# Fixed order of the last value projections: weights two units ahead, four decay buffers, output-weight halves in the gate stage, key norms one unit on

## The chip, the cores and the metric

The kernel runs on one core of one Trainium2 chip. The metric is the device time of one execution in microseconds (us). Before the change the median of three executions is 2239.89 us (2238.68 to 2241.77).

## The reference

One inference step of a two-layer streaming encoder, over 2048 prompt tokens and 32 sample tokens (2080 in all), width 1024: a gated delta layer, then a layer of sliding-window attention. Only the first layer's input side matters here:

```python
A_HEADS = 8; A_DK = A_DV = 128; CONV_W = 4
proj = x @ w_in                       # q, k, v: 24 rows of 128 features; gate z: 8 rows; decay and beta: 16 columns
qkv, conv_state = causal_conv(proj[..., :3072], buf, w)   # 4 taps per feature, then SiLU
q, k = l2norm(q), l2norm(k)
gcum = jnp.cumsum(g, axis=-1)
decay = jnp.exp(jnp.where(incl, gcum[..., :, None] - gcum[..., None, :], -jnp.inf))
# ... chunks of tokens: (I + lower)^-1, recurrence over chunks, o
out = (rms_norm(o) * silu(z)) @ w_out
```

## The kernel before

All large matrix products are made in three passes: each operand is split into a high part (a rounded copy, made on ACT) and a low part (the difference, made on POOL or DVE), and `project` multiplies hi by hi, hi by lo and lo by hi over eight slices of 128 (lines 74 to 82).

**Units.** A unit is one of the 24 rows of 128 features of q (0 to 7), k (8 to 15) and v (16 to 23), over all 2080 tokens in five blocks of 416. A block is 24 matmuls into one PSUM buffer, which ACT copies into the row R (`block`, line 294); a unit is 120 matmuls. There are six such PSUM buffers. `conv` (line 196) is a generator that turns the finished row of the unit before into its convolved, activated form on ACT and DVE: a scaled copy on ACT (L204), three multiply-adds on DVE (L207), a tanh on ACT (L211), a last DVE pass (L213), then the stores to scratch on SP's queue (L216, L218); for q and k also squares, a transpose and a sum (L221 to L224), and behind the last key unit the norms of all keys (`norms`, with its table of logarithms, some 40 small DVE instructions and eight matmuls at L456).

**Weights.** `fetch_weights` (L47) loads a unit's 512 KB into the one buffer `w_raw`; `split_fetched` makes `w_hi` on ACT (L54) and `w_lo` on POOL (L55), two buffers each.

**Orders.** The rest of the program around this is put in order by a list scheduler. Units 0 to 15 are free (FREE = 15). From unit 16 on, `ordered` (L230) fixes the order of TensorE, DVE, ACT and SP to that in which the code issues: per unit the fetch of the next unit's weights, then per block one step of the decay table, some steps of `conv`, and the block; the next weights are split behind block 0, and behind block 2 comes one output-weight half.

**Decays.** `decays` (L260) makes the exponentials of the differences of cumulative gates, 17 token tiles of two head groups, so 34 steps: a broadcast load into E (L271), a mask added on DVE (L280), four exponentials on ACT (L284), a store (L285). Three places serve as E in turn, and a step's load goes out one step ahead.

**Output weights.** `split_out_weights` (L1074) splits a_w_out once into hi and lo halves kept in scratch, 16 steps of a load (256 KB, L1080), a cast on ACT (L1081), a subtraction on POOL (L1082) and a store (512 KB, L1083), through the buffer `th`, which `conv` uses too. Eight steps stand in units 7 to 14, eight in units 16 to 23.

**Gate stage.** `z` (L301) makes the eight rows of the gate for blocks 0 to 2; it yields after every six matmuls, four times a block, 96 steps in all. Thirteen steps are interleaved with the convolution of unit 23, then 15 follow, then `Ahead.inverses` begins, which needs k, E and other tables from scratch and makes the inverses of the first two chunks: key products on TensorE (L669), then a chain of small DVE instructions (L703, L705), interleaved with gate steps. TensorE and DVE have a fixed order there; ACT, POOL and SP are scheduled. Gate rows leave through `keep_gate` on SP (L328, L333).

Of the kernel before, what the change touches and what calls it, by code (L numbers as in the profile page):

```python
# [10 lines left out]
F32 = mybir.dt.float32  # L11
# [8 lines left out]
ET = mybir.EngineType  # L20
# [71 lines left out]
def drain(gen):  # L92
    for _ in gen:
        pass


class P1:
# [50 lines left out]
    def qkv(self):  # L148
        nc, I, T, G, big, one = self.nc, self.I, self.T, self.G, self.big, self.one
        G["triu"] = one.tile([128, 128], F32, tag="triu", name="triu")  # L150
        nc.sync.dma_start(G["triu"][:], I["triu"])
        G["ones"] = one.tile([128, 128], F32, tag="ones", name="ones")
        nc.gpsimd.memset(G["ones"][:], 1.0)
        gtmp = one.tile([128, 8, NTT, H], F32, tag="gtmp", name="gtmp")
        G["cc"] = gtmp[:, 3]
        abT = gtmp[:, 0:2].rearrange("p a t h -> p (a t h)").rearrange("p (t c) -> p t c", c=16)
        abr = one.tile([48, NT], F32, tag="th", name="abr")
        nc.gpsimd.memset(abT[:, NTT - 1, :], 0.0)
        wab = self.wab
        Rs = [self.row(0), self.row(1)]  # L160
        for b in range(NB):
            ps = self.ps()
            xh, xl = self.x[b]
            for k in range(KC):
                nc.tensor.matmul(ps[:48, :TB], wab[:, k, :48], xh[:, k, :], start=(k == 0), stop=False,
                                 skip_group_check=True)
                nc.tensor.matmul(ps[:16, :TB], wab[:, k, :16], xl[:, k, :], start=False, stop=(k == KC - 1),
                                 skip_group_check=True)
            nc.scalar.copy(abr[:, b * TB:(b + 1) * TB], ps[:48, :TB])
            for t in range(b * TB // 128, NTT if b == NB - 1 else (b + 1) * TB // 128):  # L170
                n = min(128, NT - t * 128)
                tp = self.pt.tile([128, 512], F32, tag="tp", name="tp")
                nc.tensor.transpose(tp[:n, :48], abr[:, t * 128:t * 128 + n], G["ident"][:48, :48])
                nc.vector.tensor_copy(abT[:n, t, :], tp[:n, 32:48])
                nc.vector.tensor_tensor(out=abT[:n, t, :], in0=abT[:n, t, :], in1=tp[:n, :16], op=ALU.add)
            for i in range(2):
                self.block(Rs[i], self.w0[i], b)
        gates(nc, I, T, G, abT, gtmp, one, self.pt)
        parts = one.tile([128, 8, NT // 32], F32, tag="parts", name="parts")
        wo = split_out_weights(nc, one, "th", I["a_w_out"], T["wo"])  # L180
        for i in range(self.FREE + 1):
            if i < 2:
                R = Rs[i]
            else:
                w = split_weights(nc, self.wp, I["w_in"][i], nc.gpsimd)
                R = self.row(i)
                for b in range(NB):
                    self.block(R, w, b)
            if 7 <= i < self.FREE:
                next(wo)  # L190
            if i < self.FREE:
                drain(self.conv(i, R, parts))
        with self.tc.manual_schedule(engines={ET.PE, ET.DVE, ET.Activation, ET.SP}):
            self.ordered(R, parts, wo)

    def conv(self, i, R, parts):

# [29 lines left out]
        if h == 7:  # L227
            norms(nc, self.G, parts, self.sel, kind, one, self.pt)

    def ordered(self, R, parts, wo):  # L230

        nc, I = self.nc, self.I
        w = split_weights(nc, self.wp, I["w_in"][self.FREE + 1], nc.gpsimd)
        matrices = None
        for i in range(self.FREE + 1, 24):
            c = self.conv(i - 1, R, parts)
            nxt = self.row(i)
            raw = fetch_weights(nc, self.wp, I["w_in"][i + 1])
            next(c)
            for b in range(NB):  # L240
                if matrices:
                    next(matrices, None)
                for _ in range((2, 2, 1, 1, 0)[b]):
                    next(c, None)
                if b == 3:
                    next(wo)
                self.block(nxt, w, b)
                if b == 0:
                    following = split_fetched(nc, self.wp, raw, nc.gpsimd)
            drain(c)  # L250
            R, w = nxt, following
            if i == self.FREE + 1:
                matrices = self.decays()
                next(matrices)
        self.room = self.one, ("parts", "gtmp")
        self.tail = self.conv(23, R, parts)
        next(self.tail)
        self.w24 = w

    def decays(self):  # L260

        nc, G, T = self.nc, self.G, self.T
        nm = self.one.tile([128, 128], F32, tag="triu", name="nm")
        nc.sync.dma_start(nm[:], self.I["nm"])
        todo = [(t, q) for t in (NTT - 1, *range(NTT - 1)) for q in range(2)]

        def load(m):
            t, q = todo[m]
            n, hs = min(128, NT - t * 128), slice(q * 4, q * 4 + 4)
            E = self.one.tile([128, 4, 128], F32, tag=("parts", "sel", "gtmp")[m % 3], name="E")  # L270
            nc.sync.dma_start(E[:, :, :n], T["gcum"][t, hs, :n].partition_broadcast(128))  # L271
            return E, t, n, hs

        ahead = load(0)
        yield
        for m in range(len(todo)):
            E, t, n, hs = ahead
            if m + 1 < len(todo):
                ahead = load(m + 1)
            nc.vector.tensor_tensor(out=E[:n, :, :n], in0=E[:n, :, :n],  # L280
                                    in1=nm[:n, :n].unsqueeze(1).to_broadcast([n, 4, n]), op=ALU.add)
            for j in range(4):
                h = hs.start + j
                nc.scalar.activation(E[:n, j, :n], E[:n, j, :n], AF.Exp, bias=G["ngc"][:n, t, h:h + 1])  # L284
            nc.sync.dma_start(T["E"][t, :n, hs, :n], E[:n, :, :n])  # L285
            yield

    def row(self, i):
# [782 lines left out]
        yield  # L1071


def split_out_weights(nc, pool, tag, src, kept):  # L1074

    for k in range(kept.shape[1]):
        for c in (slice(0, D // 2), slice(D // 2, D)):
            t = pool.tile([128, 3, D // 2], F32R, tag=tag, name="wo_parts")
            raw = t[:, 0].bitcast(F32)
            nc.sync.dma_start(raw, src[k][:, c])  # L1080
# [560 lines left out]
def program(tc, I, O, T, G):  # L1641
    nc = tc.nc
# [16 lines left out]
    chunks[0].pool = zp  # L1659
    ahead = Ahead(tc, mid, left, I, O, T, G).inverses(chunks[:2])  # L1660
    next(ahead)
    with tc.manual_schedule(engines={ET.PE, ET.DVE}):
        for _ in range(15):
            next(z)
        for i, _ in enumerate(ahead):
            if i < 8 or i % 2:
                next(z, None)
        drain(z)
    w = p1.first_gate(nc.gpsimd)
    raw = p1.late_raw(zp, 1)  # L1670
    mid.close()
# [225 lines left out]
```

## Time and profile before

| | |
|---|---|
| median of three executions | 2239.89 us |
| the profiled execution | 2244.03 us, span 2242.2 us |
| TensorE matmul busy | 2158.0 us, 96% of the span |
| VectorE (DVE), ScalarE (ACT), GpSimd (POOL) busy | 62%, 40%, 37% |
| mean granted TensorE clock | 0.985 |
| DMA, mean over the span | 137 GB/s |
| units 16 to 23 and the first gate steps | about 399 to 681 us of the span |

How to read the rows: times are us from the start of the span; "L54" is a line of the kernel; `out<-in` names tiles; a bracket at the end of a row gives how long the engine sat idle before it and which instruction, on which engine, ended the wait. SPq rows are DMA issues in the order of SP's queue. In rows of stretches, the count in parentheses is of instructions; a few matmul records can be missing. PEld is the load of a stationary operand, which overlaps the matmuls.

### The profile page before, as it was taken

Reading aid. Unit: us, or ns where it says so; the run is one execution under the profiler, and the core shown is the slowest. Engines: PE = TensorE matmul, PEld = TensorE weight load, DVE = VectorE, ACT = ScalarE, POOL = GpSimd, SP = SyncE. Lnnn points to the kernel's source line nnn. Section 1 sums busy time; section 2 is a strip of 40 time slices with the busy share of each in tenths; the row PEclk is TensorE's granted clock in tenths of the full one; section 3 lists DMA queues with packets and bytes.
Section 4 is the critical chain, followed back from the end, with each engine's and each line's share of the span. In section 5 each row is a group of like instructions: output and inputs, shape, how many; then the busy total and the mean of one; then the engine's idle time right before and its main releaser. Section 6 shows DMA issues by size and latency. Waiting matters only on the chain.

```text
span 2242.2 us, 36907 instructions
## 1 busy us (share of the span) xinstructions
PE 2158.0 (96%) x13690; PEld 1988.5 (89%) x13690; DVE 1387.3 (62%) x2718; ACT 899.4 (40%) x2273; POOL 833.9 (37%) x1185
## 2 busy tenths in 40 slices
PE   8999999988788999999999999999999999999998
PEld 6999999988788999999988888999999987787885
DVE  3666666744556668888887886224543225768775
ACT  4344444344441266666762212312112235544442
POOL 1422132111121157777750111236432124555654
PEclk9999999998899999999999999999999999999999
DMA  5222233254546535445765664455212277333321
GB/s 194 67 70 83 93 115 99 75 170 152 159 145 164 160 127 165 152 164 163 261 223 178 215 210 129 147 182 198 82 65 78 74 190 257 85 85 104 95 71 52
DMA packets 268116, 308.29 MB, mean 137 GB/s; under 512 B 79728, under 2 KB 198832, under 8 KB 267664
## 3 DMA queue, kind: packets, MB, share of 16 engines
q1 hardware_dynamic: 256688, 282.45, 40.6%
q10 hardware_dynamic: 11248, 23.48, 3.2%
q8 instruction: 108, 1.77, 0.3%
q14 instruction: 72, 0.59, 0.1%
HBM read 189.63 MB, written 116.60 MB: 137 GB/s over the span
## 4 chain that ended last, share of the span: by engine, by line
PE 63%; DVE 3%; DMA 2%; ACT 1%; issue 1%; SPq 0%; POOL 0%; DVEq 0%; ACTq 0%; POOLq 0%
PE ps L78 8%; PE ps L80 8%; PE ps L79 8%; PE po L1118 5%; PE po L1120 5%; PE po L1119 5%; PE ot L1611 4%; PE S L1590 2%; PE tr L1605 2%; PE g L669 1%; PE ks L811 1%; PE gq L796 1%; PE sp L811 1%; PE vp L811 1%; PE op L841 1%; PE op L835 1%
## 5 line engine op out<-in xcount | busy, mean ns | idle before, releaser
L78 PE MATMUL ps<-act_hi,w_hi 128*128 128x416 f32 x2000 | 715.4, 358 | 21.9 <-ACT w_hi L54 19.4
L80 PE MATMUL ps<-act_hi,w_lo 128*128 128x416 f32 x2000 | 713.3, 357 | 21.8 <-POOL w_lo L55 21.8
L79 PE MATMUL ps<-act_lo,w_hi 128*128 128x416 f32 x2000 | 708.7, 354 | 0.4 <-DVE act_lo L70 0.4
L78 PEld LDWEIGHTS ps<-act_hi,w_hi 128*128 128x128 f32 x2000 | 381.8, 191 | 30.7 <-ACT w_hi L54 22.3
L80 PEld LDWEIGHTS ps<-act_hi,w_lo 128*128 128x128 f32 x2000 | 381.2, 191 | 29.1 <-POOL w_lo L55 24.6
L79 PEld LDWEIGHTS ps<-act_lo,w_hi 128*128 128x128 f32 x2000 | 381.7, 191 | 5.6 <-DVE act_lo L70 0.9
L55 POOL TENSOR_TENSOR w_lo<-w_raw,w_hi 128x1024 fp32r<-128x1024 f32 x44 | 130.4, 2964 | 471.0 <-ACT w_hi L54 435.2
L207 DVE SCALAR_TENSOR_TENSOR y<-R,convw,y 128x2083 f32<-128x2083 f32 x72 | 181.7, 2524 | 43.2 <-ACT y L204 29.5
L1598 POOL TENSOR_TENSOR P<-P,sm 128x384 f32<-128x384 f32 (+2 forms) x128 | 100.5, 807 | 174.2 <-DVE sm L1476 105.5
L703 POOL TENSOR_TENSOR tm<-L,Tt 128x60 f32<-128x60 f32 (+19 forms) x365 | 124.5, 341 | 99.3 <-issue 40.2
L705 POOL TENSOR_TENSOR Tt<-Tt,tm 128x60 f32<-128x60 f32 (+19 forms) x365 | 143.7, 394 | 28.6
L1472 ACT ACTIVATE P<-S,nm 128x192 f32<-128x192 f32 (+3 forms) x260 | 104.6, 418 | 90.6 <-DVE nm L1465 43.9
L1118 PE MATMUL po<-wo_hi,g_hi 128*128 128x512 f32 x256 | 103.5, 404 | 0.0
L299 ACT COPY R<-ps 128x416 f32<-128x416 f32 (+1 forms) x144 | 60.1, 443 | 105.0 <-PE ps L80 94.0
L1120 PE MATMUL po<-wo_hi,g_lo 128*128 128x512 f32 x256 | 100.3, 392 | 0.6 <-DVE g_lo L1161 0.6
L1119 PE MATMUL po<-wo_lo,g_hi 128*128 128x512 f32 x256 | 100.0, 391 | 0.0
L1316 POOL TENSOR_TENSOR rs<-rs,sin 128x416 f32<-128x416 f32 x50 | 70.7, 1415 | 78.5 <-DVE rs L1315 72.2
L1611 PE MATMUL ot<-pt,vd 128*128 128x256 f32 x372 | 97.2, 388 | 1.6 <-ACT pt L1607 1.1
L280 DVE TENSOR_TENSOR E<-E,nm 128x512 f32<-128x512 f32 (+1 forms) x34 | 37.6, 1105 | 95.2 <-DMA s_E<-E 66.3
L1118 PE MATMUL po<-wo,g_hi 128*128 128x512 f32 x224 | 93.0, 415 | 0.0
L1401 DVE SCALAR_TENSOR_TENSOR za<-zs,za 128x416 f32<-128x416 f32 x40 | 32.2, 808 | 94.9 <-ACT za L1400 94.8
L1120 PE MATMUL po<-wo,g_lo 128*128 128x512 f32 x224 | 90.1, 402 | 0.0
(304 smaller groups left out, 4089.7 us busy)
## 6 DMA issues: line engine op xcount, KB each, us to landing
w_raw<-in_w_in SPq DMA_DIRECT2D x40, 512.0 KB
w_raw<-in_b_w_in SPq DMA_DIRECT2D x20, 512.0 KB
k<-s_k SPq DMA_DIRECT2D x17, 512.0 KB
E<-s_E SPq DMA_DIRECT2D x17, 512.0 KB
s_bz<-za SPq DMA_DIRECT2D x40, 208.0 KB
s_bq<-ra SPq DMA_DIRECT2D x40, 208.0 KB
s_q<-y SPq DMA_DIRECT2D x8, 1024.0 KB
s_wo<-wo_parts SPq DMA_DIRECT2D x16, 512.0 KB
```

What stands on the lines that cost most here:

```text
L55: sub.tensor_tensor(out=lo[:], in0=raw[:], in1=hi[:], op=ALU.subtract)
L78: nc.tensor.matmul(ps, hi[:, k, :], xh[:, k, :], start=(k == 0), stop=False)
L79: nc.tensor.matmul(ps, hi[:, k, :], xl[:, k, :], start=False, stop=False)
L80: nc.tensor.matmul(ps, lo[:, k, :], xh[:, k, :], start=False, stop=(k == KC - 1))
L207: nc.vector.scalar_tensor_tensor(out=y[:], in0=R[:, j:j + W], scalar=self.convw[:, i, j:j + 1], in1=y[:], op0=ALU.mult, op1=ALU.add)
L703: P.tensor_tensor(out=tm[:n, i0 - k:, :w], in0=L[:n, i0:, j:j + 1].to_broadcast(sh), in1=Tt[:n, j:j + 1, :w].to_broadcast(sh), op=ALU.mult)
L705: P.tensor_tensor(out=Tt[:n, i0:, :w], in0=Tt[:n, i0:, :w], in1=tm[:n, i0 - k:, :w], op=ALU.subtract)
L1118: nc.tensor.matmul(ps[:n], ghi[:, k, :n], w[0][:, k, cs], start=a, stop=False)
L1119: nc.tensor.matmul(ps[:n], ghi[:, k, :n], w[1][:, k, cs], start=False, stop=False)
L1120: nc.tensor.matmul(ps[:n], glo[:, k, :n], w[0][:, k, cs], start=False, stop=z)
L1472: nc.scalar.activation(P[u], src, AF.Exp, bias=nm[:, u:u + 1], scale=1.0, accum_out=sm[:, u:u + 1])
L1611: nc.tensor.matmul(ot[:, p], self.vd[:, kc0 + j, p, :], pt[:, 2 * j:2 * j + 2, :], start=(j == 0), stop=(j == nj - 1))
```

## The change

Weights: the fetch for unit i + 2 is issued before block 2 of unit i, and the split of unit i + 1's weights stands at the start of unit i. Decays: a fourth place for E (`gtmp` is made into two), loads three steps ahead, issued behind the step's store; the steps start in unit 17 at block 1, and two units take a second step at block 3. The norms of the keys, which were drained at the end of unit 16, are drained in unit 17 before block 1. Output-weight halves leave the fixed order: nine now stand in units 6 to 14, and seven in the gate stage with two buffers of their own. POOL's order is fixed as well in `ordered`, and 18 instead of 15 gate steps stand ahead of the inverses.

```diff
         parts = one.tile([128, 8, NT // 32], F32, tag="parts", name="parts")
-        wo = split_out_weights(nc, one, "th", I["a_w_out"], T["wo"])
+        self.parts = one, "th"
+        self.wo = split_out_weights(nc, self, I["a_w_out"], T["wo"])
...
-            if 7 <= i < self.FREE:
-                next(wo)
+            if 6 <= i < self.FREE:
+                next(self.wo)
...
-        with self.tc.manual_schedule(engines={ET.PE, ET.DVE, ET.Activation, ET.SP}):
-            self.ordered(R, parts, wo)
+        with self.tc.manual_schedule(engines={ET.PE, ET.DVE, ET.Activation, ET.SP, ET.Pool}):
+            self.ordered(R, parts)
...
         w = split_weights(nc, self.wp, I["w_in"][self.FREE + 1], nc.gpsimd)
+        raw = fetch_weights(nc, self.wp, I["w_in"][self.FREE + 2])
         matrices = None
         for i in range(self.FREE + 1, 24):
             c = self.conv(i - 1, R, parts)
             nxt = self.row(i)
-            raw = fetch_weights(nc, self.wp, I["w_in"][i + 1])
+            following = split_fetched(nc, self.wp, raw, nc.gpsimd)
             next(c)
             for b in range(NB):
-                if matrices:
+                for _ in range(2 if i in (self.FREE + 3, self.FREE + 4) and b == 3 else 1 if matrices else 0):
                     next(matrices, None)
                 for _ in range((2, 2, 1, 1, 0)[b]):
                     next(c, None)
-                if b == 3:
-                    next(wo)
+                if b == 2 and i < 23:
+                    raw = fetch_weights(nc, self.wp, I["w_in"][i + 2])
+                if i == self.FREE + 2 and b == 1:
+                    drain(last)
+                    matrices = self.decays()
+                    next(matrices)
                 self.block(nxt, w, b)
-                if b == 0:
-                    following = split_fetched(nc, self.wp, raw, nc.gpsimd)
-            drain(c)
+            last = c
             R, w = nxt, following
-            if i == self.FREE + 1:
-                matrices = self.decays()
-                next(matrices)
...
         nm = self.one.tile([128, 128], F32, tag="triu", name="nm")
+        both = self.one.tile([128, 2, 4, 128], F32, tag="gtmp", name="E")
...
-            E = self.one.tile([128, 4, 128], F32, tag=("parts", "sel", "gtmp")[m % 3], name="E")
+            if m % 2:
+                E = both[:, m // 2 % 2]
+            else:
+                E = self.one.tile([128, 4, 128], F32, tag=("parts", "sel")[m // 2 % 2], name="E")
...
-        ahead = load(0)
+        ahead = [load(0), load(1), load(2)]
         yield
         for m in range(len(todo)):
-            E, t, n, hs = ahead
-            if m + 1 < len(todo):
-                ahead = load(m + 1)
+            E, t, n, hs = ahead.pop(0)
...
             nc.sync.dma_start(T["E"][t, :n, hs, :n], E[:n, :, :n])
+            if m + 3 < len(todo):
+                ahead.append(load(m + 3))
             yield
...
-def split_out_weights(nc, pool, tag, src, kept):
+def split_out_weights(nc, room, src, kept):
...
+            pool, tag = room.parts
...
+    p1.parts = new_pool(tc, mid, "p1_wo", 2, side="right"), "wo_parts"
     with tc.manual_schedule(engines={ET.PE, ET.DVE}):
-        for _ in range(15):
+        for _ in range(18):
             next(z)
         for i, _ in enumerate(ahead):
             if i < 8 or i % 2:
                 next(z, None)
+            if i % 16 == 8:
+                next(p1.wo, None)
         drain(z)
+        drain(p1.wo)
```

In the orders below the lines of the changed kernel are a few higher (E's load is L276, its store L288, the value row's stores L217 and L219, the exponentials L287, the output-weight load and store L1086 and L1089). SP's queue in a unit of the fixed order, before, from one fetch of weights to the next:

```order
L47 DMA w_raw<-in_w_in 128x1024
...
L285 DMA s_E<-E 128x512
L216 DMA s_v<-y 128x16x128
L218 DMA s_v<-y 128x32
L1080 DMA wo_parts<-in_a_w_out 128x512
L1083 DMA s_wo<-wo_parts 128x2x512
L271 DMA E<-s_gcum 128x512
L285 DMA s_E<-E 128x512
L47 DMA w_raw<-in_w_in 128x1024
```

and with the change:

```order
L47 DMA w_raw<-in_w_in 128x1024
L288 DMA s_E<-E 128x512
L276 DMA E<-s_gcum 128x512
L288 DMA s_E<-E 128x512
L276 DMA E<-s_gcum 128x512
L217 DMA s_v<-y 128x16x128
L219 DMA s_v<-y 128x32
L288 DMA s_E<-E 128x512
L276 DMA E<-s_gcum 128x512
```

The output-weight load and store are gone from between the value row's stores and the decay loads, and a block's load of E now follows its store.

ACT's order around the cast of a unit's weights in the same part, before:

```order
L284 ACTIVATE E<-E,t_ngc 128x128 x4
L1081 CAST wo_parts<-wo_parts 128x512
L299 COPY R<-ps 128x416
L284 ACTIVATE E<-E,t_ngc 128x128 x4
L299 COPY R<-ps 128x384
L299 COPY R<-ps 128x32
L204 ACTIVATE y<-R,convw 128x2083
L284 ACTIVATE E<-E,t_ngc 128x128 x4
L299 COPY R<-ps 128x416
L54 CAST w_hi<-w_raw 128x1024
```

and with the change:

```order
L287 ACTIVATE E<-E,t_ngc 128x128 x4
L304 COPY R<-ps 128x384
L304 COPY R<-ps 128x32
L54 CAST w_hi<-w_raw 128x1024
L205 ACTIVATE y<-R,convw 128x2083
L287 ACTIVATE E<-E,t_ngc 128x128 x4
L304 COPY R<-ps 128x416
```

The cast has moved ahead of the convolution's first step and of the unit's first exponentials, right behind the copies of the row before (384 and 32 are the two pieces of its last block).

SP's queue from the last value row's store to the loads of the inverses, before:

```order
L216 DMA s_v<-y 128x16x128
L218 DMA s_v<-y 128x32
L333 DMA s_z<-z 128x64
L328 DMA s_z<-z 128x2x128
L333 DMA s_z<-z 128x96
L627 DMA tinit<-in_tinit 128x256
L640 DMA k<-s_k 128x1024
L640 DMA k<-s_k 128x8x32
```

and with the change:

```order
L217 DMA s_v<-y 128x16x128
L219 DMA s_v<-y 128x32
L47 DMA w_raw<-in_w_in 128x1024
L338 DMA s_z<-z 128x64
L333 DMA s_z<-z 128x2x128
L338 DMA s_z<-z 128x96
L632 DMA tinit<-in_tinit 128x256
L645 DMA k<-s_k 128x1024
L648 DMA E<-s_E 32x8x32
L1086 DMA wo_parts<-in_a_w_out 128x512 x2
L645 DMA k<-s_k 128x8x32
```

A fetch of gate weights, an E and two output-weight halves now stand ahead of the small load of k, which the first key product needs.

More of the change, by code (lines that the diff above doesn't have):

```diff
@@ L228, in conv, with ordered @@
             norms(nc, self.G, parts, self.sel, kind, one, self.pt)
-    def ordered(self, R, parts, wo):
+    def ordered(self, R, parts):
         nc, I = self.nc, self.I
         w = split_weights(nc, self.wp, I["w_in"][self.FREE + 1], nc.gpsimd)
+        raw = fetch_weights(nc, self.wp, I["w_in"][self.FREE + 2])
         matrices = None
```

## The prediction

> **What bounds the kernel now.** I first read who waited for whom on TensorE (waited for: us in total, times, longest), since it is busy 96% of the span.
>
> ```profile
> PE ps L80 <- POOL w_lo L55: 21.8, 7, 3.6
> PE ps L78 <- ACT w_hi L54: 19.4, 7, 3.7
> PE g L669 <- DMA k<-s_k: 11.1, 3, 9.5
> ```
>
> TensorE waits some 41 us for split weights and 11 us for one load of keys; what else it waits for is small. Next the busy times by stretch, cut where units begin (columns: PE, PEld, DVE, ACT, POOL busy with counts, granted clock, DMA share, GB/s).
>
> ```profile
> 60.00:420.00 360.00, 360.00 (x1917) 353.14 (x1916) 246.49 (x151) 156.42 (x203) 97.85 (x86) 1.00 0.29 88
> ...
> 474.00:480.00 6.00, 5.39 (x16) 5.21 (x17) 4.55 (x4) 3.79 (x7) 1.09 (x3) 0.50 0.31 77
> ```
>
> ```profile
> 446.40:470.30 23.90, 22.62 (x121) 22.14 (x119) 6.94 (x6) 11.62 (x26) 1.60 (x3) 1.00 0.61 179
> 470.30:502.00 31.70, 25.84 (x120) 24.85 (x120) 14.68 (x10) 13.77 (x30) 6.33 (x6) 0.89 0.53 159
> ...
> 598.30:630.40 32.10, 25.46 (x121) 24.47 (x121) 13.90 (x10) 13.77 (x30) 5.58 (x7) 0.89 0.49 153
> 630.40:654.30 23.90, 19.96 (x96) 18.97 (x96) 11.02 (x6) 10.02 (x21) 9.33 (x4) 0.86 0.57 159
> 654.30:681.00 26.70, 17.20 (x90) 16.76 (x90) 16.58 (x14) 8.98 (x13) 4.00 (x4) 0.89 0.55 159
> 681.00:700.00 19.00, 18.97 (x102) 18.21 (x103) 12.17 (x24) 3.42 (x6) 2.40 (x1) 0.88 0.72 193
> 700.00:785.00 85.00, 85.00 (x480) 84.14 (x479) 60.84 (x162) 18.14 (x32) 14.10 (x18) 1.00 0.48 145
> ```
>
> From 60 to 420 us TensorE runs gapless at clock 1.00. From 470 us each unit of the same 120 matmuls takes some 32 us. After 700 us it is gapless again. So all that this change can win lies between 470 and 700 us. The loss in a unit has two halves: idle time, and the clock, which is 0.50 for some 7 us behind the idle time (0.11 of 32 us is 3.5 us). Then the order of time, TensorE first (last bracket: idle before, and what ended it), and the casts that mark an undisturbed unit.
>
> ```profile
> 421.74 2.09 PE L456 MATMUL n_ps<-parts,sel 128*128 128x136 f32 x8 [0.70 <-DVE parts L224]
> ...
> 470.34 0.46 PE L78 MATMUL ps<-act_hi,w_hi 128*128 128x416 f32 x1 [1.33 <-ACT w_hi L54]
> 474.61 0.72 PE L80 MATMUL ps<-act_hi,w_lo 128*128 128x416 f32 x1 [3.63 <-POOL w_lo L55]
> ...
> 630.35 0.45 PE L78 MATMUL ps<-act_hi,w_hi 128*128 128x416 f32 x1 [3.75 <-ACT w_hi L54]
> ...
> 681.03 0.64 PE L669 MATMUL g<-k 128*32 128x32 f32 x8 [9.50 <-DMA k<-s_k]
> ```
>
> ```profile
> 353.09 1.06 ACT L54 CAST w_hi<-w_raw 128x1024 fp32r<-128x1024 f32 x1 [3.34 <-PE ps L79]
> ...
> 375.69 1.05 ACT L54 CAST w_hi<-w_raw 128x1024 fp32r<-128x1024 f32 x1 [3.34 <-PE ps L79]
> ```
>
> The two casts are one unit apart: 22.60 us. Unit 16 ends at 421.74 - 0.70 = 421.04; 470.34 is the start of unit 19 and 630.35 that of the first gate head. Why w_hi and w_lo come late is told by SP's queue, then ACT, POOL and DVE, around 455 to 475 us.
>
> ```profile
> 454.86 1.23 SPq L1080 DMA_DIRECT2D wo_parts<-in_a_w_out  x1
> 460.99 0.37 SPq L1083 DMA_DIRECT2D s_wo<-wo_parts  x1
> 461.46 0.41 SPq L271 DMA_DIRECT2D E<-s_gcum  x1
> ...
> 462.66 0.44 SPq L47 DMA_DIRECT2D w_raw<-in_w_in  x1
> ```
>
> ```profile
> 458.97 0.62 ACT L1081 CAST wo_parts<-wo_parts 128x512 fp32r<-128x512 f32 x1 [7.18 <-DMA wo_parts<-in_a_w_out]
> ...
> 461.65 2.05 ACT L204 ACTIVATE y<-R,convw 128x2083 f32<-128x2083 f32 x1
> 467.68 1.28 ACT L284 ACTIVATE E<-E,t_ngc 128x128 f32<-128x128 f32 x4 [3.98 <-DVE E L280]
> ...
> 469.25 1.04 ACT L54 CAST w_hi<-w_raw 128x1024 fp32r<-128x1024 f32 x1
> ```
>
> ```profile
> 459.67 1.29 POOL L1082 TENSOR_TENSOR wo_parts<-wo_parts 128x512 fp32r<-128x512 f32 x1 [13.58 <-ACT wo_parts L1081]
> ...
> 470.37 4.19 POOL L55 TENSOR_TENSOR w_lo<-w_raw,w_hi 128x1024 fp32r<-128x1024 f32 x1 [8.46 <-ACT w_hi L54]
> ```
>
> ```profile
> 466.95 0.69 DVE L280 TENSOR_TENSOR E<-E,nm 128x512 f32<-128x512 f32 x1 [13.36 <-DMA s_E<-E]
> ```
>
> It is one loop through four in-order engines. SP issues the output-weight half's load at 454.86; its store can go only at 460.99, after ACT's cast and POOL's subtraction. Only then come the next decay block's load and the weights' fetch (462.66). DVE gets that decay block at 466.95, ACT its exponentials at 467.68, and the weights' cast stands behind them in ACT's order: 469.25. TensorE needed it at 469.0. The loop takes 502.00 - 470.30 = 31.7 us, a unit needs 22.6: TensorE is paced by it, 9 us lost per unit.
>
> **The change part by part.**
>
> Output-weight halves leave the fixed order: eight go (one into the free part, seven into the gate stage). That takes 461.46 - 454.86 = 6.6 us of SP's standstill out of each loop. The one in the free part costs ACT 0.62 and POOL 1.29 us, where they are busy 156 and 98 of 360 us under a gapless TensorE: nothing.
>
> Weights two units ahead: the fetch goes out in the middle of a unit for the unit after next, and the cast leads each unit's ACT work instead of following an exponential. It needs a whole unit's lead to fail before TensorE waits: from fetch to cast at most 6.6 us (462.66 to 469.25, an upper bound, as ACT was busy elsewhere), cast 1.04, subtraction 4.19.
>
> Four decay buffers: a load is issued three blocks ahead (three blocks of 4.5 us) and needs the store of one block ago to have landed, so DVE's waits for E should go.
>
> Key norms one unit on: they sit on DVE behind three convolution passes of unit 17.
>
> ```profile
> 423.87 0.30 DVE L459 TENSOR_SCALAR n_x<-n_ps 128x136 f32<-128x136 f32 x1 [2.18 <-PE n_ps L456]
> ...
> 435.51 0.30 DVE L447 TENSOR_TENSOR t_ngc<-t_ngc,n_lx 128x136 f32<-128x136 f32 x1
> ...
> 467.56 4.81 DVE L207 SCALAR_TENSOR_TENSOR y<-R,convw,y 128x2083 f32<-128x2083 f32 x2
> ```
>
> They are the tightest spot, so I follow it by hand. Unit 16 ends at 421.04; copies, cast and convolution start (0.5, 1.0, 2.05) end at 424.6, three passes of 2.4 at 431.8, norms (11.9) at 443.7, the first E and its exponentials (2) at 445.7. SP puts that E's store ahead of the fetch for unit 19: fetch 446.6, raw there by 453.2, cast 454.2, subtraction 458.4. Unit 19 begins at 421.04 + 2.09 + 2 x 22.60 = 468.3: 9.9 us to spare. Norms cost TensorE their 2.09 us as before; were that cover gone, the excess would be paid once.
>
> Can the other engines keep 22.6 us? The rows of a unit give DVE 14.7, ACT 13.8 - 0.6 = 13.2, POOL 6.3 - 1.3 = 5.0 us. DMA: 0.51 of 32 us is 16.3; a half's 0.75 MB at 159/0.53 = 300 GB/s is 2.5; the 13.8 left is a share of 0.61, which unit 18 (446.4 to 470.3) had without starving TensorE until its end. So units 17 to 23 should run gapless. **The first gate head starts at 421.04 + 2.09 + 7 x 22.60 = 581.3 instead of 630.35: 49.0 us.**
>
> Gate stage up to the first keys: before, 13 + 15 = 28 gate steps (six matmuls, a twentieth of a unit, 1.13 us: 31.6 us) took 681.03 - 630.35 = 50.7 us. That is 19.0 lost to late weights, half clock and the 9.5 us for k. Now 31 steps stand there, 35.0 us. Is k in time?
>
> ```profile
> 670.21 0.37 SPq L216 DMA_DIRECT2D s_v<-y  x1
> ...
> 676.23 1.10 SPq L640 DMA_DIRECT2D k<-s_k  x2
> ```
>
> From the last value row's store to k's arrival it took 681.03 - 670.21 = 10.8 us; the new SP order puts four more issues between them (a weight fetch, E, two output-weight loads: 2.0 us at 0.5). That store is ready some 16.6 us after the stage begins: 3.6 to the convolution's first step, 4.8 for two passes, 1.3 for a gate block, 2.4, then 2.2 and 2.3 for another block and the last pass. So k lands at 29.4, 5.6 us before it is needed. If the cover goes: between nothing and the old 9.5 + 3.5 us. I take nothing. **The 19.0 us are won.** The three steps moved forward are missing later, so they cancel.
>
> The half clock behind the k wait (681 to 700 us, 0.12 x 19) is worth 0 to 2.3 more; I leave it against small waits that I cannot price.
>
> Seven halves in the gate stage: ACT 7 x 0.62 = 4.3, POOL 7 x 1.29 = 9.0, DMA 5.3 MB = 18 us at 300 GB/s, beside 85 us in which ACT is busy 18, POOL 14, and DMA 0.48: hidden as long as SP does not hold up gate stores. DVE is the close one, 60.84 of 85 us. Beside POOL's subtraction an E add took 2.83 us, not 0.68, and the subtraction 4.19, not 2.41:
>
> ```profile
> 472.28 2.83 DVE L280 TENSOR_TENSOR E<-E,nm 128x512 f32<-128x512 f32 x1
> ...
> 477.33 0.68 DVE L280 TENSOR_TENSOR E<-E,nm 128x512 f32<-128x512 f32 x1
> ```
>
> ```profile
> 639.31 2.41 POOL L343 TENSOR_TENSOR w_lo<-w_raw,w_hi 128x1024 fp32r<-128x1024 f32 x1 [4.73 <-ACT w_hi L351]
> ```
>
> So a subtraction may hold DVE for its length: bounds 0 and 9.0 us, 69.8 of 85 us at most, still under TensorE: nothing. The Trainium skill, "SBUF — State Buffer", section "Who interferes with whom", says that a VectorE instruction with two SBUF inputs and a GpSimd one that reads SBUF exclude each other for the whole instruction, whoever comes first. By that rule the full 9.0 us fall on DVE, and a stage that DVE paced would end 9.0 us later; the rows above agree with it in kind.
>
> Sum: 49.0 + 19.0 = **68.0 us**. The profiled execution took 2244.03 us for its span of 2242.2, so it would take 2176.0; it lies 4.1 over the median, 2239.89, which becomes **2171.9, say 2172**. Behind 785 us the engines' orders are unchanged.
>
> **The rivals.**
>
> A: the decay chain still paces. Without the halves the loop is 31.7 - 6.6 = 25.1 us, if the four buffers win nothing. For it: convolution, exponentials and casts are one serial chain on ACT and DVE (the row x2 of 4.81 us, 2.83 for an E add beside POOL). Against: the cast no longer stands behind an exponential of its own unit. Five units times 2.5 us is 12.5 lost: 2184.
>
> B: the gate stage gives back. The halves' loads stand in SP's queue before the small k, and a store waiting for POOL holds back gate stores and weight fetches. Against: six PSUM buffers (27 us of blocks) stand between TensorE and the stores. Price: the old k wait and its half clock, 9.5 + 3.5 = 13 us, or DVE's 9.0: 2181 to 2185.
>
> C, slower: each of the seven halves stops the gate stage as it stopped the units, 31.7 - 22.6 = 9.1 us, since the same load, cast, subtraction, store sequence stands in SP's queue, and the k wait stays: 63.7 + 9.5 = 73.2 against 68.0, 2245. It decides from 9.7 us per half. Against: no exponential waits behind it there.
>
> D: the lead is in name only. One raw buffer remains, so a fetch waits for POOL's subtraction of the previous weights; if those slipped a whole unit, the loop would stay: 2240.
>
> **How the numbers follow.** Forecast 0.68 (own range 2166 to 2178: the 2.3 us of clock and 2 us of spread above, 6 us of small waits), A 0.13, B 0.12, C 0.05, D 0.02. The range 2166 to 2190 takes in A and B. Over 0.2% (4.5 us, about what a measurement can tell from no change) faster: forecast, A and B, 0.93; within: D, 0.02; slower: C, 0.05.
>
> **What would show it.** Windows of 22.6 us with 120 matmuls at clock 1.00 from 424 to 581 us; w_hi and w_lo gone from TensorE's waits; the E waits gone from DVE's; the first key product near 616 us without a wait; about 85 us of gapless TensorE behind it. Units of 25 us mean A, a wait on k or a clock of 0.5 in the gate stage means B, gaps between gate heads C. I would be wrong altogether if the gapless stretch brought a lower clock by itself, which 360 us at 1.00 speak against.

## The result, and the profile after

| | before | after |
|---|---|---|
| median (lowest to highest), 4 executions each | 2240.83 us (2238.68 to 2242.36) | 2173.12 us (2169.78 to 2174.22) |
| the profiled execution, its span | 2244.03 us, 2242.2 us | 2172.59 us, 2170.7 us |
| start of the gate stage | 630.35 us | 580.8 us |
| first key product of the inverses | 681.03 us | 619.23 us |

The ratio is 0.9696, with a 95% interval of 0.9679 to 0.9713: 67.7 us faster, where 67.9 (2239.89 to 2172) were predicted. The page of the changed kernel, busy times:

```profile
PE 2136.9 (98%) x13690; PEld 1973.4 (91%) x13690; DVE 1369.1 (63%) x2718; ACT 898.9 (41%) x2273; POOL 837.7 (39%) x1185
```

Who waited for whom on TensorE (waited for: us in total, times, longest):

```profile
PE ps L78 <- ACT w_hi L54: 2.3, 1, 2.3
...
PE ps L80 <- POOL w_lo L55: 1.1, 1, 1.1
...
PE g L674 <- DMA k<-s_k: 0.8, 1, 0.8
```

Before, w_lo, w_hi and k headed this list with 21.8, 19.4 and 11.1 us (20.7, 16.2 and 9.5 of them between 421 and 720 us). What is left of them lies elsewhere in the program: restricted to the time from 60 to 720 us, this view is empty. The busy times by stretch (PE, PEld, DVE, ACT, POOL with counts, granted clock, DMA share, GB/s), first before, cut at the start of the gate stage and at the first key product, then after, cut at the same events, with a stretch of about one unit in between:

```profile
421.00:630.30 209.30, 175.29 (x849) 169.21 (x848) 101.96 (x93) 88.22 (x191) 39.34 (x41) 0.91 0.49 149
630.30:681.00 50.70, 37.20 (x186) 35.78 (x186) 27.69 (x20) 19.00 (x34) 13.34 (x7) 0.87 0.56 160
681.00:785.00 104.00, 103.97 (x580) 102.35 (x581) 73.02 (x185) 21.56 (x38) 16.50 (x19) 0.98 0.53 154
```

```profile
421.00:580.80 159.80, 159.80 (x848) 158.57 (x847) 99.21 (x97) 89.63 (x199) 36.11 (x33) 1.00 0.58 173
580.80:619.20 38.40, 38.40 (x205) 37.97 (x204) 19.61 (x18) 13.28 (x19) 11.18 (x7) 1.00 0.62 169
619.20:720.00 100.80, 100.80 (x577) 99.29 (x577) 68.86 (x182) 24.09 (x45) 23.70 (x24) 1.00 0.64 200
...
470.00:492.00 22.00, 22.00 (x119) 21.85 (x118) 13.51 (x10) 14.22 (x33) 5.27 (x5) 1.00 0.71 207
```

The same 848 matmuls took 209.3 us and now 159.8, without a gap and at clock 1.00. The middle row needs care: 186 matmuls stood between the start of the gate stage and the first key product before, 205 now (a matmul or two can be missing from either).

The order of time in the changed kernel, at the spot that the prediction followed by hand and then in the gate stage:

```profile
443.77 0.28 DVE L283 TENSOR_TENSOR E<-E,nm 32x128 f32<-32x128 f32 x1
...
445.97 0.38 SPq L47 DMA_DIRECT2D w_raw<-in_w_in  x1
...
450.65 1.05 ACT L54 CAST w_hi<-w_raw 128x1024 fp32r<-128x1024 f32 x1 [1.16 <-DMA w_raw<-in_w_in]
...
451.78 2.42 POOL L55 TENSOR_TENSOR w_lo<-w_raw,w_hi 128x1024 fp32r<-128x1024 f32 x1 [19.41 <-ACT w_hi L54]
...
580.82 1.05 ACT L356 CAST w_hi<-w_raw 128x1024 fp32r<-128x1024 f32 x1 [3.42 <-PE ps L79]
...
597.17 0.37 SPq L217 DMA_DIRECT2D s_v<-y  x1
...
606.99 0.60 SPq L645 DMA_DIRECT2D k<-s_k  x1
...
619.23 0.44 PE L674 MATMUL g<-k 128*32 128x32 f32 x8
```

The cast at 580.82 waited for the last unit's matmuls to release its buffer, so it marks the start of the gate stage. The last row has no bracket: TensorE reached the key product without waiting for k.

**Where the 67 us are.** The gate stage starts 49.55 us earlier (630.35 - 580.8). Behind it, the same 31 gate steps took 50.7 us before, 15.7 more than their 35.0 (31 x 1.13); now 34 steps take 38.4, which is 34 x 1.13. From the first key product to a common point a little behind (the scaled keys on ACT, at 786.40 before and 719.40 now) it was 105.4 us and is 100.2: 3.4 of these 5.2 are the three steps that moved ahead; the other 1.8 are put down to the half clock that followed the wait for k, as TensorE has no gap there in either. Sum: 49.55 + 15.7 + 1.8 = 67.0, which is 786.40 - 719.40. The two spans differ by 4.5 us more, which arose in three places further on: 0.9 near 1080 us of the kernel before, 1.9 near 1410 and 1.8 near 1830, where this execution of it waited longer (1.47 us instead of 0.49 for a split activation, 3.27 instead of 2.32 for second-layer weights). The medians, 67.7 apart, do not have it.

### The profile page after: what moved, and what is told of

Same layout as the page of the kernel before. It is cut to its first block, busy times and chain, and to the rows that moved or that the text cites. A ratio compares the mean times of both kernels' runs of the same rounds, so it can differ in the third digit from the quotient of the medians.

```text
span 2170.7 us, 36895 instructions
## 1 busy us (share of the span) xinstructions
PE 2136.9 (98%) x13690; PEld 1973.4 (91%) x13690; DVE 1369.1 (63%) x2718; ACT 898.9 (41%) x2273; POOL 837.7 (39%) x1185
## 4 chain that ended last, share of the span: by engine, by line
PE 93%; DVE 3%; DMA 2%; ACT 1%; issue 0%; POOL 0%; ACTq 0%; DVEq 0%; POOLq 0%
PE ps L78 17%; PE ps L80 17%; PE ps L79 17%; PE po L1124 5%; PE po L1126 5%; PE po L1125 5%; PE ot L1617 4%; PE S L1596 2%; PE tr L1611 2%; PE g L674 1%; PE ks L816 1%; PE gq L801 1%; PE sp L816 1%; PE op L840 1%; PE vp L816 1%; PE op L846 1%
## 5 line engine op out<-in xcount | busy, mean ns | idle before, releaser
L78 PE MATMUL ps<-act_hi,w_hi 128*128 128x416 f32 x2000 | 706.4, 354 | 3.0 <-ACT w_hi L54 2.3
L80 PE MATMUL ps<-act_hi,w_lo 128*128 128x416 f32 x2000 | 705.0, 353 | 1.3 <-POOL w_lo L55 1.1
L79 PE MATMUL ps<-act_lo,w_hi 128*128 128x416 f32 x2000 | 701.2, 351 | 0.4 <-DVE act_lo L70 0.4
L78 PEld LDWEIGHTS ps<-act_hi,w_hi 128*128 128x128 f32 x2000 | 376.8, 189 | 8.8 <-ACT w_hi L54 3.1
L80 PEld LDWEIGHTS ps<-act_hi,w_lo 128*128 128x128 f32 x2000 | 375.9, 188 | 6.3 <-POOL w_lo L55 1.6
L79 PEld LDWEIGHTS ps<-act_lo,w_hi 128*128 128x128 f32 x2000 | 376.1, 188 | 5.0 <-DVE act_lo L70 0.8
L55 POOL TENSOR_TENSOR w_lo<-w_raw,w_hi 128x1024 fp32r<-128x1024 f32 x44 | 117.0, 2658 | 474.0 <-ACT w_hi L54 437.7
L1126 PE MATMUL po<-wo_hi,g_lo 128*128 128x512 f32 x256 | 100.2, 391 | 0.6 <-DVE g_lo L1167 0.6
L54 ACT CAST w_hi<-w_raw 128x1024 fp32r<-128x1024 f32 x48 | 50.4, 1050 | 101.9 <-PE ps L79 74.6
```

Source lines behind the costliest of these rows:

```text
L55: sub.tensor_tensor(out=lo[:], in0=raw[:], in1=hi[:], op=ALU.subtract)
L78: nc.tensor.matmul(ps, hi[:, k, :], xh[:, k, :], start=(k == 0), stop=False)
L79: nc.tensor.matmul(ps, hi[:, k, :], xl[:, k, :], start=False, stop=False)
L80: nc.tensor.matmul(ps, lo[:, k, :], xh[:, k, :], start=False, stop=(k == KC - 1))
L1126: nc.tensor.matmul(ps[:n], glo[:, k, :n], w[0][:, k, cs], start=False, stop=z)
```

## The experiments

The kernel before ran beside each batch: 2241.64 us for the first four, 2241.02 for the next, 2241.87 for the last. Ratios are to it.

**1. Only the halves leave the fixed order** (before, with this part alone):

```diff
...
-                if b == 3:
-                    next(wo)
...
+            if i % 16 == 8:
+                next(p1.wo, None)
```

> The kernel before with one part of the change: the output-weight halves leave the fixed order (nine in units 6 to 14, seven in the gate stage); weights, decays, norms and the 15 gate steps stay as before. Loop theory (halves, decay loads and the late cast share one loop of 31.7 us): the loop becomes 31.7 - 6.6 = 25.1 us, units 19 to 23 start 25 us apart, some 12 us stay lost, and the late convolution keeps a part of the key wait: 2180 to 2195. Rival, the halves are the whole cause: units of 22.6 us, 2173 to 2176. Rival, the halves matter little beside the late weights: 2220 or more.

Measured: 2190.97 us (2189.89 to 2193.71), ratio 0.9782 [0.9767, 0.9796]. TensorE's first low product of each unit, and windows of 2 us behind three of those:

```profile
494.06 0.71 PE L80 MATMUL ps<-act_hi,w_lo 128*128 128x416 f32 x1 [2.15 <-POOL w_lo L55]
519.59 0.46 PE L80 MATMUL ps<-act_hi,w_lo 128*128 128x416 f32 x1 [1.13 <-POOL w_lo L55]
545.46 0.71 PE L80 MATMUL ps<-act_hi,w_lo 128*128 128x416 f32 x1 [3.01 <-POOL w_lo L55]
571.21 0.45 PE L80 MATMUL ps<-act_hi,w_lo 128*128 128x416 f32 x1 [1.41 <-POOL w_lo L55]
```

```profile
494.10:496.00 1.90, 1.90 (x6) 1.82 (x7) 1.90 (x2) 1.28 (x4) 0.00 (x0) 0.50 0.00 0
...
519.60:521.60 2.00, 2.00 (x11) 1.99 (x12) 2.00 (x2) 1.28 (x4) 0.00 (x0) 1.00 0.00 0
...
545.50:547.50 2.00, 2.00 (x6) 1.92 (x7) 2.00 (x2) 1.28 (x4) 0.00 (x0) 0.50 0.00 0
```

Units are (571.21 - 494.06) / 3 = 25.7 us apart: this is rival A's loop (25.1), running, and the time lies in the range that was expected (2180 to 2195). Of the 3.1 us that a unit loses, the waits are 1.9 (mean of the four rows); most of the rest is the clock of 0.50 behind the longer ones. The wait for k is gone.

**2. Only the weights two units ahead** (before, with this part and POOL's fixed order):

```diff
+        raw = fetch_weights(nc, self.wp, I["w_in"][self.FREE + 2])
...
-            raw = fetch_weights(nc, self.wp, I["w_in"][i + 1])
+            following = split_fetched(nc, self.wp, raw, nc.gpsimd)
...
+                if b == 2 and i < 23:
+                    raw = fetch_weights(nc, self.wp, I["w_in"][i + 2])
                 self.block(nxt, w, b)
-                if b == 0:
-                    following = split_fetched(nc, self.wp, raw, nc.gpsimd)
```

> The kernel before with one part of the change: weights fetched two units ahead and split at the start of a unit, POOL's order fixed too; halves, decays, norms and gate steps stay as before. Loop theory: ACT and DVE still take some 31 us for a unit, so TensorE runs ahead by what the earlier weights and six PSUM buffers allow, and then waits later: the last value row is no earlier, k lands as late as before, and TensorE waits there instead: 2230 to 2242. Rival, TensorE only lacked the weights: units of 22.6 us, 49 us won: 2190.

Measured: 2224.57 us (2221.91 to 2226.94), ratio 0.9928 [0.9912, 0.9945]: outside both expected ranges, between them and nearer the loop's. Its waits on TensorE:

```profile
PE ps L78 <- ACT R L300: 26.3, 10, 5.6
PE g L670 <- DMA k<-s_k: 10.8, 3, 9.0
```

The wait for weights is gone and another has taken its place: TensorE now runs out of PSUM buffers, since ACT's copies out of them come late. Units are still some 29.3 us apart.

**3. Only the four decay buffers** (before, with `decays` of the changed kernel):

```diff
-        ahead = load(0)
+        ahead = [load(0), load(1), load(2)]
...
-            E, t, n, hs = ahead
-            if m + 1 < len(todo):
-                ahead = load(m + 1)
+            E, t, n, hs = ahead.pop(0)
...
+            if m + 3 < len(todo):
+                ahead.append(load(m + 3))
```

> The kernel before with one part of the change: four decay buffers, loads three steps ahead and issued behind the store; halves, weights, norms and gate steps stay as before. Loop theory: DVE no longer waits some 4 us per unit for E behind the halves' standstill, so the loop falls from 31.7 to about 27: 2215 to 2225. Rival, the SP standstill alone sets the loop: 2238 to 2243.

Measured: 2216.1 us (2214.6 to 2217.66), ratio 0.9892 [0.9877, 0.9907], as expected. Units are some 27.7 us apart, TensorE waits 17.5 us for w_lo between 421 and 720 us and 7.1 for k. DVE's waits for loads of E have shrunk, and ACT's longest in this stage are for the halves' loads:

```profile
DVE E L282 <- DMA E<-s_gcum: 12.3, 6, 2.6
```

```profile
ACT wo_parts L1085 <- DMA wo_parts<-in_a_w_out: 62.8, 8, 8.8
```

**4. The change without the halves' part** (eight halves back in units 16 to 23):

```diff
...
+                if b == 3:
+                    next(self.wo)
                 self.block(nxt, w, b)
...
-            if i % 16 == 8:
-                next(p1.wo, None)
```

> The changed kernel with the output-weight halves put back into the fixed order (block 3 of units 16 to 23) and none in the gate stage. Loop theory: ACT stands some 7 us per unit waiting for the half's load, a chain of about 20 us becomes 27 to 28 us, 5 us a unit over 22.6; some 10 us of lead are used up by unit 19, then TensorE is paced and k is late: 2195 to 2210. Rival, the halves are the whole cause: 2225 or more. Rival, with weights and decays far enough ahead the halves cost nothing: 2172 to 2176.

Measured: 2222.47 us (2221.66 to 2224.07), ratio 0.9921 [0.9906, 0.9936]: above the loop's estimate, 2195 to 2210, and just short of the rival's 2225. ACT's longest waits, and one half in the order of time (SP, then ACT, which goes on to the copies that TensorE waits for):

```profile
ACT wo_parts L1089 <- DMA wo_parts<-in_a_w_out: 69.3, 8, 11.5
```

```profile
546.87 0.45 SPq L1088 DMA_DIRECT2D wo_parts<-in_a_w_out  x1
552.71 0.37 SPq L1091 DMA_DIRECT2D s_wo<-wo_parts  x1
...
550.64 0.62 ACT L1089 CAST wo_parts<-wo_parts 128x512 fp32r<-128x512 f32 x1 [9.23 <-DMA wo_parts<-in_a_w_out]
...
551.72 0.46 PE L78 MATMUL ps<-act_hi,w_hi 128*128 128x416 f32 x1 [3.53 <-ACT R L306]
```

ACT stands 9.23 us before the half's cast: 5.5 until its load is even issued (SP has the value row's two stores ahead of it), 3.8 until it has landed. ACT's copies out of PSUM stand behind that, and TensorE waits 3.53 us for one. A half costs far more than its 0.62 us on ACT because its cast stands right behind its own load.

**5 to 8. The change with one other part undone.** Weights one unit ahead again, `decays` of before, norms back at the end of unit 16, and 15 instead of 18 gate steps:

```diff
...
-                if b == 2 and i < 23:
-                    raw = fetch_weights(nc, self.wp, I["w_in"][i + 2])
...
                 self.block(nxt, w, b)
+                if b == 0:
+                    following = split_fetched(nc, self.wp, raw, nc.gpsimd)
```

```diff
...
-        ahead = [load(0), load(1), load(2)]
+        ahead = load(0)
...
```

```diff
...
+            if i == self.FREE + 1:
+                drain(c)
+                matrices = self.decays()
+                next(matrices)
```

```diff
-        for _ in range(18):
+        for _ in range(15):
```

> The changed kernel with the weights as before: fetched at a unit's start for the next unit, split behind block 0 on ACT and POOL. Loop theory: fetch (at most 6.6 us), cast and subtraction fit into one unit of 22.6 us even with ACT 8 us behind, since nothing else holds the loop: 2172 to 2180, TensorE waiting for weights a few us at most, at unit 18 or 19. Rival, the lead of two units is what removed the waits: 2195 or more.

> The changed kernel with the decays as before: three buffers, one step ahead, the load ahead of the store. Loop theory: without the halves two steps take about 8.3 us (exponentials, store and load issue, 5.5 us to E), 21 us a unit, just under 22.6; the value row's 1 MB store makes some loads later: 2173 to 2185. Rival, the four buffers carry the gain: 2200 or more.

> The changed kernel with the key norms drained at the end of unit 16 and the decays begun there. Norms stand on DVE either way for 12 us; TensorE waits under 1 us for their matmuls at the unit's end: 2173 to 2175, no difference that can be told. Rival, the norms at the unit's end hold up unit 17's convolution so that weights or rows come late: 2180 or more.

> The changed kernel with 15 instead of 18 gate steps ahead of the inverses, so that the first key product comes 3.4 us sooner. My sum: k lands with 5.6 us to spare, so 2 us are left: no difference, 2172 to 2175. Rival, k has no such cover: a wait of 1 to 4 us with its half clock, 2176 to 2181.

| undone | median (lowest to highest), us | ratio [95%] |
|---|---|---|
| weights' lead | 2171.31 (2170.39 to 2174.77) | 0.9698 [0.9678, 0.9717] |
| four decay buffers | 2182.88 (2182.33 to 2184.99) | 0.9746 [0.9731, 0.9761] |
| norms' place | 2174.15 (2171.58 to 2176.54) | 0.9705 [0.9688, 0.9722] |
| 18 gate steps | 2173.33 (2171.32 to 2176.55) | 0.9703 [0.9686, 0.9720] |

The first lies 0.7 us under the range that was expected of it, the other three within theirs. Of these four parts only the decays' matters once the rest is there, by 10 us: without it TensorE waits for PSUM copies and for k again:

```profile
593.15 0.46 PE L78 MATMUL ps<-act_hi,w_hi 128*128 128x416 f32 x1 [2.47 <-ACT R L300]
626.78 0.64 PE L670 MATMUL g<-k 128*32 128x32 f32 x8 [4.07 <-DMA k<-s_k]
```

With 15 gate steps the first key product came at 615.87 us, 35.0 us into the stage, without a wait.

**9 and 10. All sixteen halves in one place**: two in each of units 7 to 14 and none in the gate stage, or all in the gate stage.

```diff
-            if 6 <= i < self.FREE:
-                next(self.wo)
+            if 7 <= i < self.FREE:
+                for _ in range(2):
+                    next(self.wo)
...
```

```diff
...
-            if i % 16 == 8:
+            if i % 8 == 4:
                 next(p1.wo, None)
```

> The changed kernel with all sixteen output-weight halves in the free units (two each in units 7 to 14) and none in the gate stage. It asks whether the seven halves cost the gate stage anything, and whether the free part has room. Theory (they are hidden beside TensorE in both places): 2170 to 2176 us, the same as the change. Rivals B and C, as far as they hold in small: faster by what the seven halves take from the gate stage, 2160 to 2169. If the free part has less room than its busy times say (ACT 156 us of 360), slower: 9 us per half as in the fixed units would give 2220 or more.

> The changed kernel with all sixteen halves in the gate stage (every eighth step of the inverses) and none before it. It asks how far the cover of the gate stage reaches. Theory: POOL 16 x 1.29 = 20.6 us, ACT 9.9 us and 12 MB more of DMA still go beside 100 us of gapless TensorE: 2172 to 2180 us. Rival (each half holds up SP's queue of gate rows and weight fetches there too): nine more halves at 2 to 9 us each, 2190 to 2250, with TensorE waiting for w_hi or PSUM copies in the gate stage.

Measured: 2188.82 us (2187.54 to 2192.23), ratio 0.9771 [0.9757, 0.9784], and 2184.59 (2182.08 to 2185.03), ratio 0.9743 [0.9730, 0.9756]. Both miss what was expected, above the theory's range and below the rivals': neither place takes all sixteen for nothing. The first, around the start of the fixed order (ACT, POOL, TensorE):

```profile
416.97 1.95 ACT L213 ACTIVATE th<-y 128x2083 f32<-128x2083 f32 x1 [6.12 <-DMA s_wo<-wo_parts]
...
428.57 0.10 POOL L296 MEMSET R<- 128x3 f32 x1 [14.46 <-DVE parts L226]
...
428.76 2.34 POOL L55 TENSOR_TENSOR w_lo<-w_raw,w_hi 128x1024 fp32r<-128x1024 f32 x1
...
431.16 0.71 PE L80 MATMUL ps<-act_hi,w_lo 128*128 128x416 f32 x1 [8.83 <-POOL w_lo L55]
```

The halves share the buffer `th` with the convolution, whose tanh waits for a half's store; the convolutions fall behind TensorE, POOL waits for the row that the late one still holds, and the weights stand behind that. TensorE's gapless run up to 421 us had hidden a backlog that is presented at the end. The second, TensorE in the gate stage:

```profile
681.20 0.46 PE L80 MATMUL ps<-act_hi,w_lo 128*128 128x416 f32 x1 [1.79 <-POOL w_lo L346]
696.38 0.46 PE L80 MATMUL ps<-act_hi,w_lo 128*128 128x416 f32 x1 [1.38 <-POOL w_lo L55]
711.38 0.71 PE L78 MATMUL ps<-act_hi,w_hi 128*128 128x416 f32 x1 [6.00 <-DVE z L535]
```

```profile
692.00 0.62 ACT L1085 CAST wo_parts<-wo_parts 128x512 fp32r<-128x512 f32 x1 [7.42 <-DMA wo_parts<-in_a_w_out]
```

That is 9.2 us of waits, and a clock of 0.97 between 620 and 720 us makes 3 more: about the 11.5 that it lost against the change. The first two waits are for weights whose split stood behind halves on ACT and POOL, which is near to what rival B feared. The last and longest is for DVE, which was late: it had stood 2.16 us for a tanh of ACT's at 694.02, right after ACT had stood 7.42 us for a half's load, and was busy nearly throughout from then on. How the 6.0 us divide among causes was not tried. At seven halves the price is nothing, since from 619 to 720 us TensorE has no gap.

**11. Halves and decay buffers alone** (experiments 1 and 3 together, on the kernel before):

> The kernel before with two parts of the change alone: halves out of the fixed order, and four decay buffers. Weights one unit ahead, norms and gate steps as before. Theory (these two are the whole of it): 2170 to 2177 us, the same as the full change. Rival (the weights' lead or the norms' place matter once neither is there): 2180 to 2190, with TensorE waiting for w_lo.

Measured: 2175.1 us (2171.41 to 2179.33), ratio 0.9701 [0.9686, 0.9716]: no difference from the full change that can be told. These two parts make up all of the gain that can be told.

**12. A half's load issued ahead of its cast** (experiment 4, with the load in block 3 and the rest in block 0 of the next unit):

```diff
...
             nc.sync.dma_start(raw, src[k][:, c])
+            yield
             nc.scalar.copy(t[:, 1], raw)
...
+                if b == 3 or b == 0 and i > self.FREE + 1:
+                    next(self.wo)
                 self.block(nxt, w, b)
```

> The changed kernel with eight halves back in units 16 to 23, but a half's load is issued in block 3 and its cast, subtraction and store stand in block 0 of the next unit, some 9 us later. With cast right behind the load this cost 50 us (2222), and ACT stood 8.7 us per half waiting for the load. Theory (what cost was ACT standing for the load in its fixed order, and the exponentials, copies and casts behind it): most of the 50 us are back, 2172 to 2185. Rival (SP's standstill for the store, or the place in the order as such): 2200 or more, with TensorE still waiting in each unit.

Measured: 2176.8 us (2174.57 to 2178.67), ratio 0.9709 [0.9697, 0.9722]. ACT's wait for the halves, one half in the order of time, and the stretch up to the gate stage:

```profile
ACT wo_parts L1092 <- DMA wo_parts<-in_a_w_out: 17.1, 7, 6.0
```

```profile
546.72 0.84 SPq L1090 DMA_DIRECT2D wo_parts<-in_a_w_out  x1
...
554.18 0.37 SPq L1094 DMA_DIRECT2D s_wo<-wo_parts  x1
...
550.36 0.62 ACT L1092 CAST wo_parts<-wo_parts 128x512 fp32r<-128x512 f32 x1 [1.35 <-DMA wo_parts<-in_a_w_out]
```

```profile
421.00:580.80 159.80, 159.80 (x849) 158.56 (x848) 103.37 (x95) 89.34 (x195) 55.51 (x40) 1.00 0.64 200
```

The halves are in the units, with the same casts, subtractions and transfers, and TensorE has no gap up to the gate stage; behind it, it waits 1.2 us for k. 45.7 of the 49.4 us that experiment 4 lost against the change are back. What a half cost was ACT standing for its load (69.3 us in eight, now 17.1 in seven), not its work, and not its being in the units. The cast, subtraction and store moved by two blocks along with this, so their place within a unit was not tried by itself.

## Why the prediction was right

**The loop and its end (49.0 us, measured 49.55).** Units 17 to 23 run at 22.6 us with the clock at 1.00, and the gate stage starts at 580.8 (581.3). The loop's own size held too: 25.1 us was worked out for it without the halves and with the old buffers, and experiment 1, which is that kernel, ran at 25.7. So rival A was a real loop, and what keeps it away in the change is the decays' part: 16 us between experiments 1 and 11, 10 between experiment 6 and the change. Its fourth buffer, the longer lead and the load behind the store were not tried one by one.

**What the loop consists of.** The prediction counted SP's standstill of 6.6 us per half. Experiments 4 and 12 put the emphasis elsewhere. Between them SP's wait for POOL, ahead of a half's store, fell only from 41 to 32 us (421 to 640 us), ACT's wait for the load from 69.3 to 17.1, and the time came back. The price per half came out near (31.7 - 25.7 = 6.0 us in experiment 1), as one loop has one length, but the link to cut was the cast behind its own load. Why experiment 4 (2222) is 6 us slower than experiment 3, which has fewer parts of the change, was not tried; ACT's waits for the halves are 6.5 us longer in it, which fits but is no proof.

**Weights two units ahead, and the norms.** The hand-followed spot came as written or better: first E add at 443.77 (443.7), fetch at 445.97 (446.6), cast done at 451.7 (454.2), low weights at 454.20 (458.4), needed at 468.3. The landing took 4.7 us instead of the bound of 6.6, and no add of DVE's fell beside the subtraction, so it took 2.42 and not 4.19. But this part wins nothing here: experiments 5, 7 and 11 leave the lead, the norms' place or both undone at the same time. The prediction priced the parts together and did not say this.

**Decays.** "DVE's waits for E should go" was too strong. Between 421 and 581 us they were 39.3 us for E's stores and 26.5 for its loads, and now are

```profile
DVE E L283 <- DMA E<-s_gcum: 19.5, 6, 4.4
```

which is harmless, as nothing that TensorE needs is late behind them.

**Gate stage (19.0 us): the mis-sized term.** Its step "28 gate steps took 50.7 us" left out that the inverses yield three times ahead of their first key product: 31 steps stood there before, 34 now. The loss was 50.7 - 35.0 = 15.7, and the first key product came at 619.2, not "near 616". The 1.8 us of clock behind the old wait for k, which the prediction had left aside as 0 to 2.3, made up about half of that; the total came out 1.0 us below the 68.0. That it came so near is in part luck: 3.3 us too many here, and 1.8 and 0.55 too few elsewhere, nearly cancel.

**k in time.** The last value row's store went out 16.4 us into the stage (16.6). The four issues that now stand ahead of k's small load took 4.9 us (1.19, 0.63 and 2.84, with the time between them) where 2.0 were counted, but the value row's last 16 KB took 1.79 to issue where it had taken 3.41. By the trace's record of landings the load was there at 610.84, 30.0 us into the stage (29.4). That is 8.4 us ahead of its use, as 34 steps stand there; with three fewer (experiment 8) 5.0 us were left, where 5.6 were worked out for 31 steps.

**Halves in the gate stage at nothing; rivals B, C and D.** The stretch from 619 to 720 us is gapless at clock 1.00. A stall like B's appears only with sixteen halves, at 11.5 us in all; C would have had to cost 9.7 us for each of seven; D's lead holds, though it is not needed. On B, an instruction of the inverses on DVE took 2.42 us beside a subtraction of POOL's in experiment 10, and 0.22 us otherwise:

```profile
658.29 2.42 DVE L706 TENSOR_TENSOR tm<-L,Tt 32x60 f32<-32x60 f32 x1
...
661.00 0.22 DVE L706 TENSOR_TENSOR tm<-L,Tt 32x66 f32<-32x66 f32 x1
...
657.87 2.78 POOL L346 TENSOR_TENSOR w_lo<-w_raw,w_hi 128x1024 fp32r<-128x1024 f32 x1
```

The Trainium skill, "SBUF — State Buffer", section "Who interferes with whom", has a DVE instruction with two SBUF inputs and a GpSimd one that reads SBUF exclude each other for a whole instruction; these rows agree, as DVE's instruction ended at 660.71 and POOL's at 660.65. The 9.0 us that the prediction allowed for on DVE did not reach the end of the stage, and hardly show on DVE: it was busy 68.86 of 100.8 us, and 73.02 of 104.0 before.

## What to carry to other kernels

Where an engine's order is fixed, a step "load, use, store" stops everything queued behind the use for the whole time until the load has landed: issue the load a block or two ahead of the use before moving the step elsewhere. A wait that is removed from a loop shows the next one in it (here weights, then PSUM copies, then the decay loads), so cost the loop as a whole and undo the parts one by one: two parts carried all of this change. Busy shares do not show whether a gapless stage has room: it can build up a backlog that is paid behind its end.

## What was not expected of the hardware

The clock. In experiment 1 waits of 1.13 and 1.41 us left the granted clock at 1.00 in the 2 us behind them (519.60 us above; 571.30 likewise), while one of 2.15 us halved it for some 3 us (494.10 above). The Trainium skill, "TensorE: Matmul & The Clock Gate", section "Part 1: The HAM clock gate (the "warmup" mystery)", puts the drop behind at least one idle window of about 3.4 us; here a wait shorter than that was enough, and the measurement decides for this kernel.

But the length of a wait alone does not decide. The 2.47 us in experiment 6, shown above, left the clock at 1.00:

```profile
593.20:595.20 2.00, 2.00 (x11) 1.99 (x12) 2.00 (x2) 1.46 (x5) 0.00 (x0) 1.00 0.73 265
```

In the trace's record of the granted clock, the stretches at 0.50 begin on a fixed grid of 3.41 us and last one to three of its steps (in the kernel before, up to 720 us: 6.8 or 10.2 us each). With TensorE's idle time added up per step, a clock at 1.00 fell to 0.50 behind every step with 2.09 us of idle time or more, and behind none with up to 1.86, in all traces of this case between 60 and 720 us; one at 0.50 stayed there behind every step with 0.6 us or more. The 2.47 us were cut in two by the end of a step, 0.60 and 1.86; the 2.15 us fell almost whole into one.

A small store behind a large one. SP's issue of a value row's last 16 KB took 3.48 us right behind the 1 MB store of the row, where issues beside it took 0.3 to 0.5; SP's next issue came only behind it, at 452.41. The seven such issues up to the gate stage took 3.1 to 4.8 us, the six there in the kernel before 2.1 to 2.6; why they differ is not known. In experiment 4 the same issue took 4.01 us at 542.81, just ahead of the half's load, and is a good part of ACT's 9.23 us.

```profile
448.35 0.43 SPq L217 DMA_DIRECT2D s_v<-y  x1
448.82 3.48 SPq L219 DMA_DIRECT2D s_v<-y  x1
```
